# A batched matmul: four stores held back, and the last of them issued from SP behind the last load

## The chip, the cores and the metric

The kernel runs on one core of a Trainium2 chip. The metric is the device time of one execution in microseconds (us); four runs of the kernel before have a median of 531.95 us (531.41 to 534.26). A core has TensorE (PE) for matmuls, VectorE (DVE) and ScalarE (ACT) for elementwise work, GpSimd (POOL), SyncE (SP), and 16 DMA engines. In this kernel DMAs are issued from SP and from ACT[...].

## The reference

```python
b1, b2, m, k, n = 8, 16, 256, 512, 384
x      = np.random.randn(b1, b2, m, k)   # float32
weight = np.random.randn(b1, b2, k, n)   # float32
out    = np.matmul(x, weight)            # float32
```

These are 128 independent products of 256x512 by 512x384. Read: 67 MB of x and 101 MB of weights. Written: 50 MB.

## The kernel before

The 128 batches are worked through in 65 groups (L41): 63 groups of two batches (numbered 0 to 62 here), and then two groups of one batch (63 and 64), which share one x load. For each group the program says:

- One load of x for two batches, 1024 KB (`load_x`, L58), and one load of 768 KB per weight (`load_w`, L65). All loads are issued from SP, in the order x, w, w. x has three buffers, the weights have six.
- `transpose_x` (L70): DVE casts x to bf16 (L77), PE transposes it in 128x128 blocks into PSUM (L82), DVE copies the result to SBUF (L86).
- DVE casts each weight to bf16 (L110).
- PE multiplies (L124). In a group of two batches the two matmuls of a pair work on 64 columns of the array each; a group of two has 32 matmuls, a group of one has 8 of full width.
- ACT copies the PSUM result to `out_sb` (L131), two copies for a group of two batches, one for a group of one.
- The store of `out_sb`: 768 KB for a group of two, 384 KB for a group of one.

The stores go through a list, `waiting`. In the program a group's store is issued when more than LAG = 3 groups are on the list (L138), and in the last group all stores that are left are issued after the casts and before the products (L112 to L114), and then the last group's own one. All of them are issued from ACT (L95). `out_pool` has LAG + 3 buffers (L51).

The order in which an engine gets its instructions isn't that of the program alone[...]. In the built kernel each store stands on ACT directly behind the copies of its own group, for all groups. SP holds the 192 loads and nothing else. [...]

Of the kernel before, what the change touches and what calls it, by code (L numbers as in the profile page):

```python
# [1 line left out]

# [5 lines left out]


@with_exitstack
def kernel(
    ctx: ExitStack,
    tc: tile.TileContext,
    x: bass.AP,
    weight: bass.AP,
    out: bass.AP,
):
    nc = tc.nc
    P = 128  # L20

    b1, b2, M, K = x.shape
    _, _, _, N = weight.shape
    B = b1 * b2
    KO = K // P

    x_rows = x.rearrange("b1 b2 m k -> (b1 b2 m) k")
    o_rows = out.rearrange("b1 b2 m n -> (b1 b2 m) n")
    w_flat = weight.rearrange("b1 b2 k n -> (b1 b2) k n")

    fp32 = mybir.dt.float32
    bf16 = mybir.dt.bfloat16

    GX = 2
    CX = P // GX
    R = GX * M // P


    groups = [2] * ((B - GX) // 2) + [1] * GX  # L41

    LAG = 3

    const = ctx.enter_context(tc.tile_pool(name="const", bufs=1))
    x_pool = ctx.enter_context(tc.tile_pool(name="x_pool", bufs=3))
    xb_pool = ctx.enter_context(tc.tile_pool(name="xb_pool", bufs=2))
    xt_pool = ctx.enter_context(tc.tile_pool(name="xt_pool", bufs=2))
    w_pool = ctx.enter_context(tc.tile_pool(name="w_pool", bufs=6))
    wb_pool = ctx.enter_context(tc.tile_pool(name="wb_pool", bufs=4))  # L50
    out_pool = ctx.enter_context(tc.tile_pool(name="out_pool", bufs=LAG + 3))  # L51
    psum_t = ctx.enter_context(tc.tile_pool(name="psum_t", bufs=2, space=bass.MemoryType.PSUM))
    psum_o = ctx.enter_context(tc.tile_pool(name="psum_o", bufs=3, space=bass.MemoryType.PSUM))

    identity = const.tile([P, P], bf16)
    make_identity(nc, identity)

    def load_x(b):  # L58
        x_sb = x_pool.tile([P, R, K], fp32, name="x_sb")
        nc.sync.dma_start(  # L60
            x_sb[:], x_rows[b * M : (b + GX) * M].rearrange("(p r) k -> p r k", r=R)
        )
        return x_sb

    def load_w(b):  # L65
        w_sb = w_pool.tile([P, KO, N], fp32, name="w_sb")
        nc.sync.dma_start(w_sb[:], w_flat[b].rearrange("(kp ko) n -> kp ko n", ko=KO))  # L67
        return w_sb

    def transpose_x(x_sb, RG):  # L70


        H = R // RG
        x_bf = xb_pool.tile([P, R, K], bf16, name="x_bf")
        x_t = xt_pool.tile([P, RG, KO, P, H], bf16, name="x_t")
        for r0 in range(0, R, 4):
            nc.vector.tensor_copy(out=x_bf[:, r0 : r0 + 4], in_=x_sb[:, r0 : r0 + 4])  # L77
            for r in range(r0, r0 + 4, 2):
                pt = psum_t.tile([P, 2, KO, P], bf16, name="pt")
                for rr in range(2):  # L80
                    for ko in range(KO):
                        nc.tensor.transpose(  # L82
                            pt[:, rr, ko, :], x_bf[:, r + rr, ko::KO], identity
                        )
                j = r % RG
                nc.vector.tensor_copy(  # L86
                    out=x_t[:, j : j + 2, :, :, r // RG], in_=pt[:]
                )
        return x_t

    waiting = []

    def store():
        dram, out_sb = waiting.pop(0)
        nc.scalar.dma_start(out=dram, in_=out_sb)  # L95

    b = 0
    for n, G in enumerate(groups):
        last = n == len(groups) - 1
        C = P // G  # L100
        RG = G * M // P
        if b % GX == 0:
            x_sb = load_x(b)
        w_sb = [load_w(b + i) for i in range(G)]
        if b % GX == 0:
            x_t = transpose_x(x_sb, RG)
        w_bf = []
        for i in range(G):
            t = wb_pool.tile([P, KO, N], bf16, name="w_bf")
            nc.vector.tensor_copy(out=t[:], in_=w_sb[i][:])  # L110
            w_bf.append(t)
        if last:  # L112
            while waiting:
                store()  # L114

        out_full = out_pool.tile([P, 2 * M // P, N], fp32, name="out_sb")
        out_sb = out_full[:, :RG]
        for r in range(0, RG, 2):
            po = psum_o.tile([P, 2, 512], fp32, name="po")
            for rr in range(2):  # L120
                for ko in range(KO):
                    for i in range(G):
                        c0 = (b % GX + i) * CX
                        nc.tensor.matmul(  # L124
                            po[i * C : (i + 1) * C, rr, :N],
                            x_t[:, r + rr, ko, c0 : c0 + CX, :],
                            w_bf[i][:, ko, :],
                            start=(ko == 0),
                            stop=(ko == KO - 1),
                        )  # L130
            nc.scalar.copy(out=out_sb[:, r : r + 2, :], in_=po[:, :, :N])  # L131
        waiting.append(
            (
                o_rows[b * M : (b + G) * M].rearrange("(p r) n -> p r n", r=RG),
                out_sb,
            )
        )
        if len(waiting) > LAG or last:  # L138
            store()
        b += G  # L140


# [1 line left out]
_INS = ['x', 'weight']  # L144
_OUTS = [((8, 16, 256, 384), 'float32')]


# [23 lines left out]
```

## Time and profile before

| | |
|---|---|
| median of four runs | 531.95 us |
| profiled execution: time, span from first to last instruction | 534.26 us, 532.1 us |
| mean granted TensorE clock | 0.852 |
| PE busy (matmul) | 347.4 us (65%) |
| DVE busy | 278.5 us (52%) |
| ACT busy | 103.9 us (20%) |
| HBM read, written | 167.77 MB, 50.33 MB |
| mean DMA rate over the span | 411 GB/s |
| chain that ended last | DMA 81%, PE 11%, DVE 6% |

The chain that ended last is followed back from the last instruction: at each step to what released it. The DMA share is the mean busy share of the core's 16 DMA engines. A load or a store counts as landed when all the engines that carry a part of it have reported. Besides the page, the trace keeps a record of every DMA packet (start, duration, size, queue) and of every such report; queue q1 is that of SP, q10 that of ACT.

### The profile page before, as it was taken

The page shows a single profiled execution, that of the slowest core. Times are in us where ns is not written, and L with a number is a line of the kernel's source. Part 1 is how long each engine was busy: PE and PEld are TensorE (multiplying, and loading weights), DVE is VectorE, ACT ScalarE, POOL GpSimd, SP SyncE. Part 2 cuts the span into 40 slices and gives each one's busy share as a digit, 9 for nine tenths or more (in the row PEclk, how much of TensorE's full clock was granted, in tenths as well). Part 3 has the DMA queues.
Part 4 walks back from the last instruction along what each step waited for, and adds up shares of the span by engine and source line. Part 5 has one row for each costly group of instructions (what it writes and reads, how often), then busy time and mean ns, then how long its engine had stood idle before and what let it go on. Part 6 is the DMA issues. An engine that isn't in the chain of part 4 may idle for free.

```text
span 532.1 us, 7363 instructions
## 1 busy us (share of the span) xinstructions
PE 347.4 (65%) x3056; PEld 235.7 (44%) x3056; DVE 278.5 (52%) x320; ACT 103.9 (20%) x129; POOL 0.7 (0%) x6
## 2 busy tenths in 40 slices
PE   4576585675766666657657666677656667575764
PEld 2354453454444444434435444345444444353442
DVE  4554545545555546455455554564554555455543
ACT  0221221211211211212112112122111122121211
POOL 0000000000000000000000000000000000000000
PEclk9987979869788878897887888888888888788787
DMA  8999999999999999999999999999999999999983
GB/s 345 399 425 424 424 421 423 423 421 421 426 420 423 423 422 422 422 424 422 422 422 421 424 421 422 424 421 423 422 421 424 420 423 422 422 423 421 422 358 124
DMA packets 37041, 218.59 MB, mean 411 GB/s; under 512 B 4112, under 2 KB 4112, under 8 KB 28816
## 3 DMA queue, kind: packets, MB, share of 16 engines
q1 hardware_dynamic: 27648, 167.78, 75.9%
q10 hardware_dynamic: 9360, 50.34, 22.8%
q8 instruction: 24, 0.39, 0.3%
q14 instruction: 9, 0.07, 0.0%
HBM read 167.77 MB, written 50.33 MB: 410 GB/s over the span
## 4 chain that ended last, share of the span: by engine, by line
DMA 81%; PE 11%; DVE 6%; issue 1%; DVEq 0%; ACT 0%; SPq 0%
DMA w_sb<-in_weight_dram 47%; DMA x_sb<-in_x_dram 34%; PE po L124 9%; DVE w_bf L110 3%; DVE x_t L86 3%; PE pt L82 1%; DVEq L166 0%; DVE x_bf L77 0%; ACT out_sb L131 0%; SPq L60 0%; DVEq L110 0%; SPq L67 0%; DVEq L77 0%
## 5 line engine op out<-in xcount | busy, mean ns | idle before, releaser
L124 PE MATMUL po<-w_bf,x_t 128*64 128x384 bf16 (+1 forms) x2032 | 279.6, 409 | 166.7 <-DVE w_bf L110 166.0
L124 PEld LDWEIGHTS <-x_t 128*64 128x64 bf16 (+1 forms) x2032 | 175.2, 135 | 255.3 <-DVE w_bf L110 128.3
L131 ACT COPY out_sb<-po 128x768 f32<-128x768 f32 x128 | 102.6, 801 | 424.2 <-PE po L124 424.2
L77 DVE CAST x_bf<-x_sb 128x2048 bf16<-128x2048 f32 x64 | 78.5, 1227 | 137.8 <-DMA x_sb<-in_x_dram 137.6
L110 DVE CAST w_bf<-w_sb 128x1536 bf16<-128x1536 f32 x128 | 120.1, 955 | 28.7 <-DMA w_sb<-in_weight_dram 27.4
L86 DVE COPY x_t<-pt 128x1024 bf16<-128x1024 bf16 x128 | 83.6, 696 | 78.6 <-PE pt L82 78.6
L82 PE MATMUL pt<-identity,x_bf 128*128 128x128 bf16 x1024 | 70.6, 223 | 13.9 <-DVE x_bf L77 13.6
L82 PEld LDWEIGHTS <-x_bf 128*128 128x128 bf16 x1024 | 60.5, 115 | 36.3 <-DVE x_bf L77 28.6
L131 ACT ACT_TABLE_LOAD x1 | 1.3, 1283 | 0.7 <-PEq L155 0.7
masks.py:199 POOL TENSOR_SCALAR_AFFINE_SELECT identity<-identity 128x128 bf16<-128x128 bf16 x1 | 0.3, 294 | 0.1
masks.py:197 POOL MEMSET identity<- 128x128 bf16 x1 | 0.2, 205 | 0.3 <-POOLq L155 0.3
L155 POOL MEMSET const-bfloat16-1.0<- 128x1 bf16 x1 | 0.1, 102 | 0.0
L155 POOL MEMSET const-uint8-127<- 128x1 uint8 x1 | 0.1, 102 | 0.0
L155 POOL MEMSET const-float32-0.0<- 128x1 f32 x1 | 0.1, 99 | 0.2 <-issue 0.2
L155 POOL MEMSET const-float32-1.0<- 128x1 f32 x1 | 0.1, 99 | 0.0
## 6 DMA issues: line engine op xcount, KB each, us to landing
w_sb<-in_weight_dram SPq DMA_DIRECT2D x128, 768.0 KB, 16.2
x_sb<-in_x_dram SPq DMA_DIRECT2D x64, 1024.0 KB, 16.0
out_dram<-out_sb ACTq DMA_DIRECT2D x63, 768.0 KB, 8.3
out_dram<-out_sb ACTq DMA_DIRECT2D x2, 384.0 KB, 2.3
```

Source lines behind the costliest of these rows:

```text
L77: nc.vector.tensor_copy(out=x_bf[:, r0 : r0 + 4], in_=x_sb[:, r0 : r0 + 4])
L82: nc.tensor.transpose(pt[:, rr, ko, :], x_bf[:, r + rr, ko::KO], identity)
L86: nc.vector.tensor_copy(out=x_t[:, j : j + 2, :, :, r // RG], in_=pt[:])
L110: nc.vector.tensor_copy(out=t[:], in_=w_sb[i][:])
L124: nc.tensor.matmul(po[i * C : (i + 1) * C, rr, :N], x_t[:, r + rr, ko, c0 : c0 + CX, :], w_bf[i][:, ko, :], start=(ko == 0), stop=(ko == K ...
L131: nc.scalar.copy(out=out_sb[:, r : r + 2, :], in_=po[:, :, :N])
L155: nc = _bacc.Bacc("TRN2", target_bir_lowering=False, num_devices=1)
```

## The change

LAG becomes 4, and with it the number of `out_sb` buffers 7 instead of 6. `store` takes the queue as an argument: in the last group the stores that are left are issued from SP, and all others from ACT as before.

```diff
-    LAG = 3
+    LAG = 4
...
-    def store():
+    def store(queue):
         dram, out_sb = waiting.pop(0)
-        nc.scalar.dma_start(out=dram, in_=out_sb)
+        queue.dma_start(out=dram, in_=out_sb)
...
         if last:
+
             while waiting:
-                store()
+                store(nc.sync)
...
         if len(waiting) > LAG or last:
-            store()
+            store(nc.scalar)
```

With LAG = 4 the list holds the stores of groups 60, 61, 62 and 63 when the last group comes; three of them have 768 KB, the last has 384 KB. In the built kernel these four stand on SP behind the 192nd load, in this order. Stores 0 to 59 stand on ACT where they stood before, each behind the copies of its own group; then ACT has the eight copies of groups 60 to 64 without a store among them, and store 64 at the end. The order on PE, DVE and POOL is unchanged. SP's order is the same up to these four stores, [...] the x load of group 62 now waits for the landing of store 58, and the weight load of group 63 for that of store 59, where both waited for loads before.

## The prediction

> **What bounds the kernel now.** I read the page first: its fortieths, its chain of waits, its DMA issues.
>
> ```profile
> DMA  8999999999999999999999999999999999999983
> GB/s 345 399 425 424 424 421 423 423 421 421 426 420 423 423 422 422 422 424 422 422 422 421 424 421 422 424 421 423 422 421 424 420 423 422 422 423 421 422 358 124
> ...
> w_sb<-in_weight_dram SPq DMA_DIRECT2D x128, 768.0 KB, 16.2
> ...
> out_dram<-out_sb ACTq DMA_DIRECT2D x63, 768.0 KB, 8.3
> out_dram<-out_sb ACTq DMA_DIRECT2D x2, 384.0 KB, 2.3
> ```
>
> The DMA engines are full at about 422 GB/s until the last two fortieths (13.3 us each). So the body is bound by bytes, which the change leaves alone. What it can change is the end. A store issued beside loads takes 8.3 us to land, one that meets no load 2.3 us.
>
> Next, the same chain in order of time, for its end:
>
> ```profile
> 496.97 16.22 DMA w_sb<-in_weight_dram
> ...
> 513.28 0.97 DVE w_bf L110
> ...
> 514.29 4.44 PE po L124 x30
> 518.73 0.58 PE pt L82 x8
> ...
> 520.53 0.73 DVE x_t L86
> ...
> 522.69 5.32 PE po L124 x16
> 528.01 0.02 issue
> 528.04 0.80 ACT out_sb L131
> ```
>
> I number groups from 0: 62 is the last with two batches, 63 and 64 have one each. The second weight load of group 62 (w62b) lands at 513.19; after that nothing but compute sets the end: cast, products of 62, transposes for 63/64, copies and casts, the last 16 products, copy, store.
>
> Then the timelines of ACT and DVE there (start, us, what, idle before):
>
> ```profile
> 503.43 0.34 ACTq L95 DMA_DIRECT2D out_dram<-out_sb  x1
> 509.04 0.81 ACT L131 COPY out_sb<-po 128x768 f32<-128x768 f32 x1 [0.50 <-PE po L124]
> 509.87 0.34 ACTq L95 DMA_DIRECT2D out_dram<-out_sb  x1
> ...
> 519.60 0.34 ACTq L95 DMA_DIRECT2D out_dram<-out_sb  x1
> ```
>
> ```profile
> 509.81 1.29 DVE L86 COPY x_t<-pt 128x1024 bf16<-128x1024 bf16 x2 [0.73 <-PE pt L82]
> 511.41 0.96 DVE L110 CAST w_bf<-w_sb 128x1536 bf16<-128x1536 f32 x1 [0.32 <-DMA w_sb<-in_weight_dram]
> 513.28 0.96 DVE L110 CAST w_bf<-w_sb 128x1536 bf16<-128x1536 f32 x1 [0.91 <-DMA w_sb<-in_weight_dram]
> 517.15 1.23 DVE L77 CAST x_bf<-x_sb 128x2048 bf16<-128x2048 f32 x1 [2.91 <-DMA x_sb<-in_x_dram]
> ```
>
> Every store goes out right behind its own group's second copy (509.04 + 0.81, then 509.87): the lag of three groups in the program does not survive in the built order. So store 60 left at 503.43, 61 at 509.87, 62 at 519.60, 63 at 526.30, 64 at 528.87. Stores 60 and 61 are in the engines while x63, w62b, w63 and w64 still wait there. Last, the stretches:
>
> ```profile
> 480.00:513.00 33.00, 21.87 (x194) 14.49 (x195) 17.97 (x21) 6.41 (x8) 0.00 (x0) 0.84 1.01 423
> 513.00:521.50 8.50, 5.46 (x46) 3.97 (x45) 4.35 (x4) 1.60 (x2) 0.00 (x0) 0.80 0.61 249
> 521.50:527.00 5.50, 4.31 (x14) 2.11 (x15) 2.01 (x3) 0.80 (x1) 0.00 (x0) 0.51 0.15 61
> ```
>
> (length, then busy PE, PEld, DVE, ACT, POOL; clock; DMA share; GB/s.) From 513 the DMA is only 0.61 busy though loads are pending: in the landing records the first of the 16 engines finishes w64 at 512.3, the last at 521.2. A load counts as landed with its slowest engine, and the stores sit in that engine's way.
>
> [...] in the packet records a late engine alternates ACT's ring (q10) and SP's (q1), packets starting 0.23 us apart. [...] the trace has half clock in 514.81 to 518.22 and in 521.64 to 528.46.
>
> **The change part by part.**
>
> 1. LAG 3 to 4, out_pool 6 to 7 buffers: in the built order of both kernels every instruction up to the loads of group 62 is the same, and ACT's copies wait on PE alone. Cost 0; hidden by nothing, it is simply not there. If a copy did wait for a buffer it would meet ACT, which idles 424 of 532 us.
>
> 2. Stores 60 to 63 leave ACT and stand on SP behind w64's issue; 64 stays on ACT. Four DMA issues of 0.34 us on SP, which has nothing behind them but the final wait. Each waits for its copies (60 at 503.4, 61 at 509.85, 62 at 519.57) [...]. ACT loses four issues, 1.4 us, off the path.
>
> 3. Loads become free of stores. A 768 KB store is 8 packets of 6144 B on each engine, 8 x 0.2305 = 1.84 us. On the slowest engine store 60's packets fall between x62 (landed 507.75) and w62a (511.32): x62 gains 0, w62a and w62b 1.84. So w62b lands at 513.19 - 1.84 = 511.35. x63 also loses about six packets of store 61: 1.84 + 1.38 = 3.2, to 513.8 instead of 517.05. w63 and w64 lose both stores, 3.7: 515.7 and 517.5.
>
> 4. How much of that reaches the end. [...] x_t copies of 62 until 511.10, unmoved; then the two casts, no longer waiting, 1.82 as a pair (row of groups before): 512.92. Products of 62 start in full at 512.96 instead of 514.29: gain 1.33, DVE having taken 0.5 of the 1.84. They took 4.44 at mostly half clock; at full clock 2.76 (group 61, same timeline). Before, a full clock there would have bought nothing: x63's cast ended at 518.38 and the transposes started at 518.66. After, x63's cast ends by 515.1, so the transposes start at 512.96 + 2.76 = 515.7 (full clock) or 517.3 (as in this profile). Gain 3.0 or 1.33. From there all is compute of the same length: 4.03 to the first product, w64 being there at 517.5 and needed after 519.
>
> 5. Load issue shifts. [...] the last six loads wait for others: x62 for store 58 (493.80 instead of 492.90), w63 for store 59 (505.36 instead of 503.19), the others for earlier ones. w63 goes out 2.1 later, w64 0.7. Engines that run 8 us ahead may idle; the late engine reaches w63 only after 515. Cost 0; without that backlog up to 2.1 on w63, against 2.3 of slack before (landed 519.37, cast 521.71).
>
> 6. The drain. On the late engine w64's data end at 517.1, stores 60, 61, 62 by 522.6, store 63 one more us: 523.6. Store 64 lands at 525.5 at the earliest (below). Not binding; bound 0 to +1.
>
> Sum for full clock: before, 518.66 + 4.03 + 2.65 (16 products, half of 5.30) + 0.83 + 2.33 (landing) + 0.94 = 529.45 of span; after, 3.0 less: 526.4. The profiled run is 534.26 with span 532.1, so 2.16 lie around it; 529.45 + 2.16 = 531.6 is where the three other runs lie (531.41 to 532.15). So I take the median 531.95 as a run with nearly full clock at the end, and subtract. A full-clock gain of 3.0, less an average loss of some 0.35 for the share of half clock in the products of 62, gives 2.65: **529.3 us**.
>
> **The rivals.**
> A. The clock takes it: the products of 62 run at half clock and only 1.33 arrives: 530.6. For: clock 0.85 over the span, half in this profile. [...]
> B. The loads don't come sooner, because of the later issue of w63 or because the engine that ends last is another one that had already passed its stores: 531.5 to 532. For: landing records of store 61 spread over 3.8 us. Against: store 60's packets are done at 511 on every engine, and w62b lands after.
> C. Slower: the drain becomes the bound. After w64, 2.75 MB of stores (3.5 x 786 KB) leave in one ring at the very end. It is slower by over 0.5% if store 63 lands after 531.2 + 2.7 = 533.9, so if the 2.75 MB from 517.1 move below 2.75/16.8 = 164 GB/s; at 150 GB/s the end is 535.4 + 0.9 + 2.2 = 538.5. Against: store 62 moved nearly alone at about 400 GB/s.
> D. The change doesn't act (stores end up where they were): 532. The built order excludes it.
>
> **How the numbers follow.** 0.5% of 531.95 is 2.66 us, about what a measurement of this kernel can tell from no change. Forecast (gain 2 to 4, 527.9 to 530.0): 0.57. A: 0.25. B: 0.11. C: 0.06, D: 0.01. The forecast case lies on both sides of 529.29; it gives 0.50 to faster and 0.07 to same. A, B and D are same (0.37), but for 0.01 of B with an unlucky clock, and C is slower: faster 0.50, same 0.43, slower 0.07. Range 527.8 (full clock also where the median run of before had some half clock, 4.1) to 531.4 (A whole, part of B).
>
> **What would show it.** ACT's timeline without stores between 496 and the last copy; w62b landed near 511.4, x63 near 514, w64 near 517.5; the two casts of 62 back to back at 511.1; products of 62 from 513.0; DMA share well above 0.15 in the stretch after w64; end of span near 526.5 to 529 by the clock. Wrong if w62b still lands at 513, if the last instruction waits for a store on SP's ring, or if the last products start no sooner than 521.5.

## The result, and the profile after

The changed kernel takes 529.63 us (median of 37 runs, 527.96 to 532.70), the kernel before 531.71 us (median of 58 runs beside them, 530.08 to 534.79). The ratio is 0.9963, with a 95% interval of 0.9951 to 0.9974: 2.0 us faster, between 1.4 and 2.6. (The ratios here are worked out from all runs of both kernels, so they differ a little from those of the medians.) The forecast was 529.3 in a range of 527.8 to 531.4. The gain is clear of noise and under 0.5%; the prediction had given 0.50 to a gain of more than that and 0.43 to a smaller change. The profiled run of the changed kernel has a span of 527.4 us (529.55 us as a whole).

The page of the kernel after, its fortieths (13.2 us each) and its DMA issues:

```profile
DMA  8999999999999999999999999999999999999995
GB/s 343 403 427 422 425 420 422 424 421 423 422 421 425 420 422 427 420 422 423 420 424 423 421 422 422 423 423 421 424 421 422 421 423 423 421 423 422 423 416 211
...
out_dram<-out_sb ACTq DMA_DIRECT2D x60, 768.0 KB, 8.4
out_dram<-out_sb SPq DMA_DIRECT2D x3, 768.0 KB, 10.1
```

The body is as it was. The last two fortieths moved 358 and 124 GB/s before and move 416 and 211 now: the total is the same, more of it falls in the tail, and the tail is shorter. The three big stores on SP take 10.1 us to land in place of 8.3; nothing waits for them but the end of the kernel, and they had landed before it (523.0, with the last store at 526.5).

ACT's timeline of the kernel after (start, us, what, idle before):

```profile
500.20 0.80 ACT L132 COPY out_sb<-po 128x768 f32<-128x768 f32 x1 [6.77 <-PE po L125]
502.45 0.81 ACT L132 COPY out_sb<-po 128x768 f32<-128x768 f32 x1 [1.45 <-PE po L125]
508.86 0.80 ACT L132 COPY out_sb<-po 128x768 f32<-128x768 f32 x1 [5.60 <-PE po L125]
510.20 0.80 ACT L132 COPY out_sb<-po 128x768 f32<-128x768 f32 x1 [0.55 <-PE po L125]
...
524.22 0.34 ACTq L95 DMA_DIRECT2D out_dram<-out_sb  x1
```

Stores no longer stand on ACT behind the copies that end at 503.3 and 511.0; ACT issues the last store alone. The others are on SP:

```profile
501.50 1.42 SPq L67 DMA_DIRECT2D w_sb<-in_weight_dram  x2
503.28 19.96 SPq L95 DMA_DIRECT2D out_dram<-out_sb  x4
```

Store 60 leaves at 503.28, directly behind its group's last copy; before it left at 503.43. So this store is not issued later than before. What changed is the queue that it goes into: it now stands in SP's, issued after w63 and w64 (501.50 and 501.92), where before it stood in ACT's. In the packet records of the run before, a late engine took packets from ACT's queue and SP's in turn (0.23 us apart), and store 60 was done on all 16 engines at 511.42, while w63, issued 0.17 us ahead of it, landed at 519.37. In the run after, the 16 reports of store 60, in order of time, came 1.83 to 1.90 us behind those of w64, about the 1.84 us of the store's own packets: there it came after w64, and w64 did not wait for it. Store 61 too left near its old time, at 511.03 (509.87 before).

Now the chain of waits of the kernel after, in order of time, and the stretches in which it ends:

```profile
496.95 0.97 DVE w_bf L110
...
497.97 4.44 PE po L125 x30
...
506.10 4.06 PE po L125 x30
510.16 0.58 PE pt L82 x8
...
512.06 1.75 DVE w_bf L110 x2
...
513.85 2.76 PE po L125 x30
516.61 0.58 PE pt L82 x8
...
520.58 2.79 PE po L125 x16
...
523.39 0.80 ACT out_sb L132
```

```profile
480.00:511.00 31.00, 21.89 (x192) 14.91 (x192) 15.94 (x19) 6.41 (x8) 0.00 (x0) 0.83 1.02 422
511.00:519.50 8.50, 4.47 (x52) 3.13 (x49) 6.23 (x7) 1.60 (x3) 0.00 (x0) 1.00 0.82 341
519.50:525.00 5.50, 2.77 (x16) 1.48 (x16) 1.89 (x3) 1.60 (x2) 0.00 (x0) 1.00 0.36 143
```

Before, the chain left the loads at 513.2, when w62b landed. Now it leaves them at 496.9, and the last 30 us of the chain are compute: casts, products, transposes, copies, and then the last store. In the 8.5 us from about w62b's landing (513 to 521.5 before, 511 to 519.5 now) the DMA share rose from 0.61 to 0.82, and in the next 5.5 us from 0.15 to 0.36. That is the trade the change makes: stores fill time in which the DMA engines stood half idle.

The landing of a load with its slowest engine, from the landing records of the traces (w62a and w62b are the weight loads of group 62, x63 is the x load that groups 63 and 64 share, w63 and w64 are their weights):

| us | before | after, forecast | after |
|---|---|---|---|
| w62a | 511.32 | 509.5 | 509.31 |
| w62b | 513.19 | 511.35 | 511.19 |
| x63 | 517.05 | 513.8 | 513.63 |
| w63 | 519.37 | 515.7 | 515.47 |
| w64 | 521.21 | 517.5 | 517.33 |
| last store landed | 531.19 | | 526.54 |

The last row compares more than the change. Of its 4.65 us, 2.5 are the clock in the last 16 products, 5.30 us at half clock in the profile before (0.50 from 521.64 to 528.46) and 2.77 at full in this one (1.00 to 525.85). The other 2.1 are there before these products start.

### The profile page after: what moved, and what is told of

Same layout as the page of the kernel before. It is cut to its first block, busy times and chain, and to the rows that moved or that the text cites. A ratio compares the mean times of both kernels' runs of the same rounds, so it can differ in the third digit from the quotient of the medians.

```text
span 527.4 us, 7363 instructions
## 1 busy us (share of the span) xinstructions
PE 338.2 (64%) x3056; PEld 231.6 (44%) x3056; DVE 277.9 (53%) x320; ACT 103.9 (20%) x129; POOL 0.7 (0%) x6
## 4 chain that ended last, share of the span: by engine, by line
DMA 80%; PE 12%; DVE 6%; issue 1%; SPq 1%; DVEq 0%; ACT 0%
DMA w_sb<-in_weight_dram 80%; PE po L125 10%; DVE w_bf L110 4%; DVE x_t L86 3%; PE pt L82 1%; DVEq L167 0%; SPq L67 0%; SPq L60 0%; ACT out_sb L132 0%; DVEq L110 0%
## 5 line engine op out<-in xcount | busy, mean ns | idle before, releaser
L125 PE MATMUL po<-w_bf,x_t 128*64 128x384 bf16 (+1 forms) x2032 | 270.5, 400 | 167.7 <-DVE w_bf L110 166.8
L125 PEld LDWEIGHTS <-x_t 128*64 128x64 bf16 (+1 forms) x2032 | 171.4, 133 | 252.1 <-DVE w_bf L110 129.0
## 6 DMA issues: line engine op xcount, KB each, us to landing
out_dram<-out_sb SPq DMA_DIRECT2D x3, 768.0 KB, 10.1
```

What stands on the lines that cost most here:

```text
L125: nc.tensor.matmul(po[i * C : (i + 1) * C, rr, :N], x_t[:, r + rr, ko, c0 : c0 + CX, :], w_bf[i][:, ko, :], start=(ko == 0), stop=(ko == K ...
```

## Experiments

Theory: store 60 sat between the last loads on every DMA engine and store 61 on the late ones (before, the first engine was done with store 60 at 510.8, with w64 at 512.3 and with store 61 at 514.1); with them gone these loads come sooner (2.0 to 3.9 us by the table), compute keeps part of it, and the drain of the stores is hidden behind the last compute. Rivals: the longer lag or the extra buffer does it; ACT freed of stores does it; any place out of the loads' way is as good; the drain is a new bound; the gain is the clock's.

**The same kernel again.** No edit.

> The changed kernel once more, beside the others on the same chip. My theory (the loads come sooner because stores 60 and 61 no longer sit between them): 0.996 of before, about 529.6 us, with w62b landed near 511.2, 1.8 to 2 us before where the kernel before has it. A rival theory that the gain was an accident of the clock: between 0.996 and 1.000 here, with no shift of the landings.

529.99 us (22 runs), ratio 0.9967, interval 0.9950 to 0.9985; w62b landed at 510.95, x63 at 513.38. The gain and the shift of the landings are there again, so neither is an accident of the clock in one set of runs.

**The lag alone.**

```diff
             while waiting:
-                store(nc.sync)
+                store(nc.scalar)
```

> LAG = 4 and seven buffers, but the last stores on ACT as before. My theory: the lag does nothing in the built order, so 1.000 of before (531.7 us, within 0.5), with store 60 issued near 503 and w62b landed near 513. Rival, that the longer lag or the extra buffer brings the gain: 529.6 us.

Ratio 1.0005, interval 0.9987 to 1.0022. The median, 532.68 us (22 runs, 530.06 to 534.69), lies 0.5 above the range that was expected; by the ratio there is no change. w62b landed at 513.08, w64 at 521.20. Its ACT timeline:

```profile
500.78 0.80 ACT L132 COPY out_sb<-po 128x768 f32<-128x768 f32 x1 [0.50 <-PE po L125]
501.61 0.34 ACTq L95 DMA_DIRECT2D out_dram<-out_sb  x1
...
510.58 0.80 ACT L132 COPY out_sb<-po 128x768 f32<-128x768 f32 x1 [1.04 <-PE po L125]
511.41 0.34 ACTq L95 DMA_DIRECT2D out_dram<-out_sb  x1
```

Each store still leaves right behind its group's last copy. The lag holds nothing back as long as the store stays on ACT; it only decides how many stores are left for SP. This run also sets the two queues side by side. Its program differs from the changed kernel's in the queue of four stores alone. Store 60 was issued at 501.61 here and at 503.28 there, and w64 landed at 521.20 here and at 517.33 there.

**The queue alone.**

```diff
-    LAG = 4
+    LAG = 3
```

> Only the queue is changed, LAG stays 3: stores 61, 62 and 63 go to SP behind the last load, store 60 stays on ACT. My theory: w62a and w62b land as before (513.2), x63, w63 and w64 come 1.4 to 1.8 sooner; the gain is 0 if the products of group 62 run at half clock and 1.5 at full, about 0.8 in the mean: 530.9 us. Rival, that what counts is ACT freed of stores or the stores' place behind the load as such: three of four stores moved, so nearly the whole gain of 2.0, 529.8 to 530.2 us.

Ratio 0.9990, interval 0.9973 to 1.0007; median 531.56 us. w62b landed at 513.09, where it was; x63 at 515.54 and w64 at 519.24, 1.5 and 2.0 sooner. Its chain of waits still leaves the loads at 513.1:

```profile
496.98 16.11 DMA w_sb<-in_weight_dram
...
513.19 0.97 DVE w_bf L110
...
514.20 2.76 PE po L125 x30
516.96 0.61 PE pt L82 x8
...
520.95 2.79 PE po L125 x16
```

Three of the four stores are moved, and about a quarter of the gain is there (0.53 us, by the interval up to 1.4; 0.8 was expected). The gain doesn't go with the number of stores taken off ACT: by the ratio most of it comes with store 60, the one in front of w62b. (The profiled run, at 529.99, is one of the fastest of the 22; it shows where the chain leaves the loads, and not the size of the gain.)

**Held back, but at the very end.** The four stores are issued from ACT after everything.

```diff
             while waiting:
-                store(nc.sync)
+            held, waiting[:] = waiting[:], []
...
+        if last:
+            for dram, o in held:
+                nc.scalar.copy(out=o[:, 0, 0:1], in_=po[:, 0, 0:1])
+                nc.scalar.dma_start(out=dram, in_=o)
```

> The four stores are held back as in the changed kernel, but they are issued from ACT at the very end, behind the last copy and the last group's own store. To keep them there, each is made to depend on the last products: one element per row of its tile is overwritten with one of the last result, so this column of the output is changed; four tiny ACT copies are added. My theory: the loads come as early as in the changed kernel (w62b near 511.2), but the 2.75 MB now drain with nothing beside them from 524 on, 7 us: 534 to 535.5 us, slower than before by 2.5 to 4. Rival, it is enough that the stores are out of the loads' way: 529.6 to 530.5 us.

537.15 us (6 runs, 535.00 to 539.20; the kernel before took 532.22 beside them, on another chip), ratio 1.0096, interval 1.0063 to 1.0129: slower than before by 5.1 us. Landings of the loads are those of the changed kernel (w62b 510.94, w64 517.06). Its stretches:

```profile
511.00:519.00 8.00, 4.29 (x48) 3.11 (x48) 5.81 (x6) 1.61 (x2) 0.00 (x0) 1.00 0.33 138
519.00:524.00 5.00, 2.77 (x16) 1.48 (x16) 0.99 (x2) 1.72 (x4) 0.00 (x0) 1.00 0.07 27
524.00:532.80 8.80, 0.00 (x0) 0.00 (x0) 0.00 (x0) 0.22 (x2) 0.00 (x0) 0.55 0.85 342
```

From 511 to 519 the DMA is a third busy and then, to 524, nearly idle (0.07); the bytes it could have moved follow when compute is over. Its own stores landed at 525.2, 527.1, 529.0, 530.9 and 531.9. So getting out of the loads' way is not enough. From the place directly behind the last load, the engines that finished their loads first began with the stores at once: in the changed kernel the first of the 16 was done with w64 at 510.2 and with store 60 at 512.1, while w64 landed at 517.3. A place in between (on ACT, but only once w64 has landed) was not tried. The price was forecast as 2.5 to 4, and the median misses that. The profiled run, at 535.0, lies in it; the median lies 2 above it, and six runs do not tell why.

**The drain left out.** The stores of groups 60 to 63 are not made.

```diff
             while waiting:
-                store(nc.sync)
+                waiting.pop(0)
```

> As the changed kernel, but the four stores of groups 60 to 63 are left out altogether, so these rows of the output are not written. My theory: in the changed kernel the drain is hidden behind the last compute, so leaving it out changes the time by no more than 0.3 us: 529.4 us. Rival, the stores behind the last load bind the end: faster by 1 us or more, 528.5 us or less.

529.57 us (22 runs, 528.15 to 532.66, on the chip of the last experiment) against 529.63 and 529.99 with the stores; fastest 528.15 against 527.96 and 528.14. The ratio, 0.9949 (0.9933 to 0.9966), overlaps with 0.9963 (0.9951 to 0.9974). By medians and fastest runs the drain of 2.75 MB costs nothing; by the ratios it is 0.7 us, with intervals wide enough for none and for more than 1 us, so the times alone don't settle it. The profiles point to none. The last store landed 2.33 us after its issue here (522.93 to 525.26) and 2.32 after it in the changed kernel (524.22 to 526.54), so the stores in front didn't hold it up. The span is 1.1 us shorter (526.3), but that arose earlier: the products of group 61 took 2.77 us in its chain, as at full clock (2.76 in the profile before), and 4.06 in that of the changed kernel.

**More stores held back.**

```diff
-    LAG = 4
+    LAG = 6      # and in another kernel 8
```

> LAG = 6: stores 58 to 63 on SP behind the last load. My theory: between LAG = 4 and LAG = 8, 528.7 us. Rival A, compute from group 60 on sets the end: 529.6 us. Rival B, the drain grows by 1.84 us per store: over 530.5 us.

528.16 us (6 runs, 527.95 to 530.41), ratio 0.9927, interval 0.9902 to 0.9952.

> LAG = 8: stores 56 to 63 on SP behind the last load. My theory: more loads come sooner, about 6.2 us per group in place of 8.05, the compute of a group takes 6.4 to 7.7, so it gains some tenths per group until the DMA engines never pause and the end is their total work: 528.2 us, the stores landing last. Rival A, the compute from group 60 on already sets the end: 529.6 us as with LAG = 4. Rival B, the drain of the stores behind the last load is the bound and grows with each of them by 1.84 us: 531 us or more.

527.96 us (7 runs, 527.79 to 528.35), ratio 0.9925, interval 0.9898 to 0.9951; in a repetition 527.96 (6 runs, 527.85 to 528.58), ratio 0.9924, interval 0.9905 to 0.9942.

> LAG = 8 with the stores on SP once more, beside the two others on the same chip: 0.9925 of before, 528.0 us, with its runs within 1 us, while those of the kernel before spread over 4 us or more.

So the gain goes on with more stores and then stops: the medians of LAG 6 and 8 are 0.2 us apart, and their intervals nearly coincide. One run with LAG = 6, the profiled one, took 530.41 us. Its last 16 products took 5.32 us, as at half clock in the profile before (5.30), where the chain of the changed kernel has 2.79:

```profile
518.72 5.32 PE po L125 x16
524.06 0.80 ACT out_sb L132
```

So with six stores compute can still set the end in a run with products as slow as these. Both rivals fall, that of compute as the bound from group 60 on, and that of a drain growing by 1.84 us per store. What ends with LAG = 8 is shown by ACT's timeline and by SP's waits in the last part of that kernel:

```profile
518.42 0.80 ACT L132 COPY out_sb<-po 128x768 f32<-128x768 f32 x1 [0.50 <-PE po L125]
519.25 0.34 ACTq L95 DMA_DIRECT2D out_dram<-out_sb  x1
```

```profile
SPq L95 <- ACT out_sb L132: 7.5, 2, 5.0
SPq L167 <- DMA out_dram<-out_sb: 6.7, 1, 6.7
```

Compute is over at 519.2, 5 us sooner than with LAG = 4 (its last copy starts at 518.42 in place of 523.39). Then SP's final wait is 6.7 us long (total, times, longest) and waits for stores: the last, that of group 63, lands at 525.17. (That of group 64, issued at 519.25, lands at 524.98, and not by 522, as the next expectation has it.) In its landing records the first of the 16 engines is done with the store of group 62 at 516.2, the last at 523.4. If the work of that last engine is the bound, one store less must show nearly in full:

```diff
         if last:
+            waiting.pop(0)
             while waiting:
                 store(nc.sync)
```

> LAG = 8 with the stores on SP, but the oldest of the eight held stores, that of group 56, is left out, so these rows of the output are not written. My theory: DMA work sets the end, so one store of 1.84 us less takes 1.8 us off, if the last store of compute (519.2 issued, 521.4 to 522 landed in the profile of LAG = 8) leaves room for it: 526.2 to 526.8 us. Rival, compute or the last store's latency sets the end: 528.0 us.

526.34 us (6 runs, 526.18 to 527.23), 1.62 below LAG = 8 on the same chip, for 1.84 of work. And compute that ends sooner must not show:

```diff
-            nc.vector.tensor_copy(out=t[:], in_=w_sb[i][:])
+            if n >= len(groups) - 4 and b % GX == 0 and i == 0:
+                nc.scalar.copy(out=t[:], in_=w_sb[i][:])
+            else:
+                nc.vector.tensor_copy(out=t[:], in_=w_sb[i][:])
```

> LAG = 8 with the stores on SP, and the first weights of groups 61, 62 and 63 cast on ACT. My theory: with LAG = 8 the slowest DMA engine never pauses before its last packet, so compute that ends earlier buys nothing: 528.0 us, and a spread of runs as narrow as with LAG = 8 (within 1 us). Rival, compute still sets the end there: about 527 us, 0.8 or more faster.

527.79 us (6 runs, 527.55 to 527.94), ratio 0.9918, interval 0.9897 to 0.9938: 0.17 below LAG = 8, with the last store issued at 516.67 in place of 519.25. Compute 2.6 us sooner bought almost nothing: with LAG = 8 the work of the slowest DMA engine sets the end.

**The same cast on ACT with LAG = 4.** The diff just shown, on the changed kernel.

> As the changed kernel, but the first weight of groups 61, 62 and 63 is cast on ACT, not on DVE. My theory: from w61b's landing on compute sets the end, with the pair of casts (1.82 us on DVE) in the chain of groups 62 and 63; one of two off DVE saves 0.85 in each: 528.2 us or the floor of the DMA work near 528. Rival, loads or the drain of the stores set the end: 529.6 us.

528.65 us (7 runs, 527.68 to 529.78), ratio 0.9938, interval 0.9917 to 0.9960. With LAG = 4 the same edit buys about 1 us by the medians (529.63 or 529.99 less 528.65) and 1.3 by the ratios. It was expected to buy more, 528.2, and its interval just touches that of the changed kernel (0.9951 to 0.9974). Its ACT and DVE timelines:

```profile
509.77 1.48 ACT L111 CAST w_bf<-w_sb 128x1536 bf16<-128x1536 f32 x1
```

```profile
509.69 1.29 DVE L86 COPY x_t<-pt 128x1024 bf16<-128x1024 bf16 x2 [0.73 <-PE pt L82]
511.48 0.96 DVE L113 CAST w_bf<-w_sb 128x1536 bf16<-128x1536 f32 x1 [0.50 <-DMA w_sb<-in_weight_dram]
```

ACT casts w62a while DVE copies, and DVE then waits half a microsecond for w62b: the chain is back at a load (w62b, 511.38), where the changed kernel had DVE casting until 513.8. So in the profile of the changed kernel the casts were on the path.

## Why the prediction was right

The prediction had the mechanism right and the size a little too large: a gain of 2.65 us was forecast and 2.0 was measured (1.4 to 2.6). The time itself came closer, 529.3 against 529.63, and in part that is luck: the forecast started from 531.95, the median of four runs, where 58 runs gave 531.71.

*Step 1 (the lag costs nothing).* Shown by the lag alone, 1.0005.

*Step 2 (the moved issues cost nothing).* The issue of the last four stores takes SP from 503.28 to 523.2, nearly all of it waiting (in SP's list 17.2 us for copies and 1.5 for loads), and only SP's final wait stands behind it.

*Step 3 (loads freed of stores).* All five landings came within 0.25 us of the forecast, in the profiled run. They follow from 8 packets of 0.2305 us per store (1.84 us; measured 1.83 to 1.90 between the reports of w64 and of store 60) and from the count of store packets ahead of each load. With store 60 put back on ACT, w62b goes back to 513.09.

*Step 4 (what reaches the end).* Two terms were mis-sized. The first is in the step's own numbers: a full clock before would have bought a little. x63's cast ended at 518.38 and the transposes started at 518.66; in the run with the lag alone they started 0.05 us after that cast. So, as an estimate from these profiles, with full clock on both sides the gain is 2.7 and not 3.0. The second is the "average loss of some 0.35 for the share of half clock in the products of 62". The step took the x_t copies of 62 as ended at 511.10, "unmoved". In the profile after they ended at 512.06, because the products of group 61 took 4.93 us from start to end, with a clock of 0.50 from 505.37 to 508.78 (505.37 to 509.00, 3.63 us, all at 1.00 in the profile before). So the products of 62 started in full at 513.85, not 512.96. Before, group 61's clock did not matter: w62b wasn't there anyway. With the loads sooner, the whole compute from group 60 on is in the chain, and every stretch at half clock in it counts. In the two profiles compared, before with the transposes of 63/64 at 518.66, after at 516.54, the part gained is 2.1. In the second profile of the changed kernel the products of 62 started in full at 513.80; where a run had the products of group 61 as short as at full clock (2.77 us, the drain left out), at 512.57, against 512.96 forecast. How often group 61 meets half clock over all runs is not shown, so that this makes up the rest of the shortfall is argued from these profiles.

*The sum.* It took the median of before as a run with nearly full clock at the end, 531.6. The fastest of the 58 runs are at 530.1, so the median probably still has some half clock in it. The gain is much the same at both ends: fastest to fastest 2.1 (530.08 to 527.96), slowest to slowest 2.1 (534.79 to 532.70).

*Step 5 (later issue of w63).* Before, x62 went out at 492.96 and w63 at 503.26, straight after loads that landed at 492.90 and 503.19, and no load waited for a store. The new waits were there, one for an x load and one for a weight load (5.8 and 4.2 us in SP's list): x62 went out at 494.99, straight after store 58 had landed at 494.92, and w63 at 501.50, straight after store 59 had landed at 501.44. The delay of w63 was not: store 59 landed 3.9 us sooner in this profile than in the one before, and w63 went out 1.8 us sooner, not 2.1 later. That leaves a rival, that loads land sooner because they are issued sooner. Three other runs answer both. With the drain left out, the stores at the end and the cast on ACT, w63 went out at 504.39, 504.90 and 505.22, later than before (503.26), and landed at 515.46, 515.21 and 515.69. With the queue alone, x63 went out 2.4 us later than before (501.90) and landed 1.5 sooner. So a late issue costs these loads nothing, as forecast, and their early landing doesn't come from an early issue.

*Step 6 and rival C (the drain).* Stores 60, 61 and 62 landed at 519.2, 521.1 and 523.0, about when the last two were issued (522.9 and 524.2). Rival C's price was real, and showed when the place behind the load was given up (1.0096). With the stores on SP the drain decides only when compute is over before the slowest engine, as with LAG = 8. One reading of the page compares two sizes: 8.3 us is a 768 KB store beside loads, 2.3 us a 384 KB store alone. Store 62 before, of 768 KB and beside the end of w64 only, took 4.3 (519.60 to 523.93). The sum doesn't rest on that reading; its 2.33 is for the 384 KB store 64.

*Rival A (half clock in the products of 62 leaves 1.33)* had the clock right and the place wrong, in this profile at least: the products of 62 ran at full clock (1.00, 2.76 us), those of 61 did not (0.50 for 3.41 us of their 4.93). What sets the clock of a stretch was not shown by any run. The measured 2.0 lies between it and 3.0. *Rivals B and D* are out by the landings.

## What to carry to other kernels

When a kernel is bound by DMA until its end, ask of each late store which loads wait behind it on the slowest DMA engine, and place it behind the last load on the same queue; here it then filled the time of the last compute. Place enough stores there to fill that time: here LAG = 8, one number changed (and with it eleven output buffers in place of seven), gives 0.9925 where 4 gives 0.9963 and 6 gives 0.9927. More than eight were not tried. Three casts moved to ACT as well give 0.9918, which is no clear difference. A hold-back written into the program is worth only what the built order keeps of it; look at the issuing engine's timeline first. And look at the queue as well as at the time: with LAG = 4 store 60 left when it always had, and only its queue was another.

## What the runs showed of the hardware that was not expected

- The 16 DMA engines drifted apart: parts of one 768 KB load, issued at one moment, were done 8.9 us apart (w64 before, 512.3 to 521.2), after a body with a mean rate of 422 GB/s. With LAG = 8 the kernel's end was that of the slowest engine: one store less took off 1.62 us, compute 2.6 us sooner 0.17.
- The spread of a kernel's runs goes with what sets its end. With compute there, it is 527.96 to 532.70 (after, 37 runs) and 530.08 to 534.79 (before, 58 runs); with DMA there, 527.79 to 528.58 (LAG = 8, 13 runs in two sets). The TensorE clock, recorded as 1.0 or 0.5 throughout (80 records in the profile before, 70 in the one after), is the likely cause of the wide ones: 30 products of a group took 2.76 us where it was 1.00 and 4.44 where it was 0.50 for most of them (before, 514.81 to 518.22), but no run held the clock fixed.
